# The later S5 parameter steps placed further on among the projections, and the first squares of x on ACT

## The chip, the cores and the metric

One core of a Trainium2 chip runs the whole program. The metric is the device time of one execution in microseconds; three executions of the kernel before were timed. PE is TensorE, DVE is VectorE, ACT is ScalarE, POOL is GpSimd, SP is SyncE, whose queue issues the loads.

## What is computed

A two-layer decoder trunk on 1024 tokens of width 1024, float32. Each layer normalises its input, projects it, runs four causal mixers of width 256 on parts of the projection, gates and merges them, projects the result and adds its norm to the input:

```python
h = _rms_norm(x, pre_g)
proj = jnp.einsum('bsd,dc->bsc', h, w_in)
...
y_ssm = s5_branch(ssm_u, ssm_a_re, ssm_a_im, ssm_log_dt, ssm_b_re, ssm_b_im, ...)
...
mix = jnp.stack([y_sb, y_ssm, y_ret, y_lru], axis=2)
mix = mix * jax.nn.silu(gates.reshape(bsz, s, N_BRANCH, BRANCH_WIDTH))
y = jnp.einsum('bsnw,nwd->bsnd', mix, w_branch)
merged = jnp.sum(jax.nn.sigmoid(merge) * y, axis=2)
return x + _rms_norm(jnp.einsum('bsd,de->bse', merged, w_out), post_g)
```

The mixers are stick-breaking attention, S5 (a complex diagonal state space with 16 groups), retention with rotary positions, and a gated linear recurrence (RG-LRU). S5 needs parameters that are worked out from `a`, `log_dt`, `b` and `c`: discretised poles, powers of them, multiplied `b` and `c`, and tables of rotations.

## The kernel before

The work is cut into four units: two layers, two chunks of 512 tokens each. A unit is a row of 64 **fillers**, which are the streamed projections: 0 to 15 make the mixers' inputs, 16 to 55 the gates, merges and branch projections (ten for each mixer), 56 to 63 the output projection. Each filler streams its weights from memory on SP's queue (`load_to`), and each half of a weight tile is split into a high part (`wh`, a copy on ACT, L86) and a low part (`wl`, a subtraction on DVE, L89), three halves ahead of its use (`split_to`, `ahead`). PE then makes three passes: high by high, low by high, high by low (`mm3`, L101). `pa` are the PSUM tiles of fillers, `pb` those of side tasks, `hh` and `hl` the split activations, `raw` the unsplit weights. `g` is any working tile of a common pool; its buffers are used in turn, so an instruction may wait until an earlier tile in the same buffer was read last.

Between the fillers run **side tasks**, written as generators: `first` (x of the first unit), `prep` (S5 parameters of a layer), `lru`, `s5`, `ret`, `sba`, `pro` (the next norm) and `post`. A hand-written table, `PLAN` (L1469), says at which half fillers of a unit each task takes its next step; an even number is before a filler, an odd one in its middle. All engines execute in the order that results, so an instruction which waits holds back everything behind it on its engine. `drain` finishes a task when a filler needs it.

`first` loads the eight tiles of x, multiplies each by its gain (ACT, L83) and makes the low part (`stt`, DVE, L98); squares of x are summed for the norm: POOL makes tiles 0 to 3 (L374) and adds them (L376), ACT makes 4 to 7, and DVE adds these four. Then POOL clears `tmat`, `ore` and `oim` (L1431).

`prep` runs on POOL for nearly all of its length (`ptt` L432, `pts` L436 and L438): exponentials, poles, their powers, `b` by the poles, then the rotation tables `tcos` and `tsin` by seven doublings, whose scratch `tmp` is a tile of the common pool. The steps behind them are:

```python
for src, dst in ((z4r, ore), (z4i, oim)):
    diag(src, dst)
...
            pe.transpose(ps[:, j * P:(j + 1) * P], src[:, 4 * h + j, :], ident)
        copy(dst[:, 4 * h:4 * h + 4, :], v3(ps[:, :], P))
```

that is two copies each into `ore` and `oim` (ACT), sixteen transposes (PE, L631) evacuated into `sre` and `sim` (ACT); then `wgh` and `wgl`, 24 products of `c` with the powers (POOL), a second `diag` of those into `ore` and `oim` (ACT), the lag matmuls (PE) and the DMAs into `tmat`. The task `s5` multiplies its input by `sre` and `sim` on PE and rotates the product by `tcos` and `tsin` on DVE, one half of the states after the other (the second half's first product writes a tile of the pool). `ret` multiplies its scores by the decay in `cons` and its queries by `xi` on DVE, multiplies both with values and states on PE for two pairs of heads in turn, and normalises the result over each head (two sums, squares on ACT, an inverse root, two products) before PE transposes it.

Of the kernel before, what the change touches and what calls it, by code (L numbers as in the profile page):

```python
# [28 lines left out]
# columns of the small parameter array  # L29
(C_CW, C_CB, C_BA, C_BX, C_LAM, C_BG, C_ARE, C_AIM, C_LDT, C_DSK, C_PG, NPAR) = (  # L30
    0, 8, 10, 12, 14, 16, 18, 26, 34, 42, 50, 58)
# columns of the constant array
# [11 lines left out]
def hybrid_kernel(ctx: ExitStack, tc: tile.TileContext, x, xt, ws1, ws2, par, bcw, preg, postg, con, rot, out, dbg=None):  # L44
# [107 lines left out]
    def group(u, i):  # L152
        # mixer of a filler in the order in which a unit takes them (LRU, S5, retention, attention by weights)
        return (0, 2, 1, 3)[(i - GATE0) // GRP] if u == 0 else (i - GATE0) // GRP

    def tile_of(u, i):
        # kind and place of the weights of a filler
        if i < GATE0:
            return 0, i
        if i >= WOUT0:  # L160
            return 0, i - 4 * 8
        n, j = group(u, i), (i - GATE0) % GRP
        return (1, 8 * n + j - 2) if j >= 2 else (0, GATE0 + 2 * n + j)
# [52 lines left out]
    S = {}  # L216

# [1 line left out]
    def prologue(u):  # L219
        l, c = units[u]  # L220
        src = x if l == 0 else x1
        gb = [G(), G()]
        xt = {}

        def load(t):
            xt[t] = [G(), G()]
            r0 = c * T + t * P
            for i in range(2):
                sp.dma_start(xt[t][i], src[r0:r0 + P, i * 512:(i + 1) * 512])

        st = smp.tile([P, 32], F32, tag="st", name=nm("st"))

        def square(t):
            junk = G(BF16)
            for i in range(2):
                actv(junk, xt[t][i], AF.Square, accum_out=st[:, 16 + 4 * i + t:17 + 4 * i + t])

        def scale(t0, n):
            # columns t0 .. t0 + n of the four blocks of st: v, 1/sqrt, scratch
            tt(st[:, t0:t0 + n], st[:, 16 + t0:16 + t0 + n], st[:, 20 + t0:20 + t0 + n], ALU.add)  # L240
            rstd(st[:, t0:t0 + n], st[:, 4 + t0:4 + t0 + n], st[:, 8 + t0:8 + t0 + n], D)

        def norm(t):
            for i in range(2):
                v = xt[t][i]
                stt(v, v, st[:, 4 + t:5 + t], gb[i], ALU.mult, ALU.mult)

        def flip(t):
            v = xt.pop(t)
            ps = [B(), B()]  # L250
            for q in range(2):
                for k in range(4):
                    pe.transpose(ps[q][:, k * P:(k + 1) * P], v[q][:, k * P:(k + 1) * P], ident)  # L253
            for q in range(2):
                pv = v3(ps[q][:, :], P)
                ho = hh[:, 4 * q:4 * q + 4, t * P:(t + 1) * P]
                copy(ho, pv)
                tt(hl[:, 4 * q:4 * q + 4, t * P:(t + 1) * P], pv, ho.bitcast(F32), ALU.subtract)
            Bdone(2)

        for t in range(NT):
            load(t)
        for i in range(2):
            sp.dma_start(gb[i], preg[l:l + 1, i * 512:(i + 1) * 512].partition_broadcast(P).rearrange("q o d -> q (o d)"))
        yield 0
        for t in range(NT):
            square(t)
            if t % 2:
                yield 0
        scale(0, 4)  # L270
        yield 0
        for t in range(NT):
            norm(t)
            if t % 2:
                yield HT + 2 if t + 1 == NT else 0
        hh = hp.tile([P, KD, T], F32R, tag="hh", name=nm("hh"))
        hl = hp.tile([P, KD, T], F32R, tag="hl", name=nm("hl"))
        for t in range(NT):
            flip(t)
            if t + 1 < NT:  # L280
                yield 2
        set_h(hh, hl)
# [4 lines left out]
    def token_rstd(acc):  # L287
        # 1/rms of token 4 p + t on partition p from sums over the other partitions
        st = smp.tile([P, 32], F32, tag="st", name=nm("st"))
        v, y, a = (st[:, 4 * i:4 * i + 4] for i in range(3))  # L290
        ps = B()
        for t in range(4):
            mm(ps[:, t:t + 1], acc[:, t:T:4], ones1)
        dve.tensor_copy(v, ps[:, 0:4])
        Bdone()
        rstd(v, y, a, D)
        return y

    def token_rows(y):
        # 1/rms of every token on all partitions  # L300
        ps = B()
        for t in range(4):
            mm(ps[:, t * P:(t + 1) * P], y[:, t:t + 1].to_broadcast([P, P]), ident)
        rb = G()
        copy(rb[:, :].rearrange("p (n t) -> p t n", t=4), v3(ps[:, :], P))
        Bdone()
        return rb

# [34 lines left out]
    def first():  # L343
# [19 lines left out]
        for k in range(KD):  # L363
# [8 lines left out]
            if k < 4:  # L372
                sqs.append(G())
                pool.tensor_tensor(sqs[k], xk[k], xk[k], op=ALU.mult)  # L374
                if k:
                    pool.tensor_tensor(sqs[0], sqs[0], sqs[k], op=ALU.add)  # L376
        S["h"] = (xh, xl)
        yield 0
        # statistics of the tokens
# [4 lines left out]
        for k in range(4, KD):  # L384
# [27 lines left out]
    def rstd(v, y, a, width):  # L412
        # v holds sums of squares; y receives 1/sqrt(mean + eps); a is scratch
# [3 lines left out]
    def rsqrt(v, y, a):  # L417
        # a bit-level first guess and three Newton steps; v becomes -v/2
# [26 lines left out]
    def exp_head(src, n, tmp):  # L445
        # 2^k factor (before its shift into the exponent) and the polynomial of the rest
# [22 lines left out]
    def prep(l):  # L469
# [18 lines left out]
        # exponentials for dt and softplus(-lambda)  # L488
# [14 lines left out]
        # discretised poles  # L503
# [20 lines left out]
        # softplus  # L524
# [30 lines left out]
        def cmul(zr, zi, ar, ai, br, bi, u1):  # L555
            # z = a * b ; u1 scratch
# [13 lines left out]
        # Bb and its multiples, for the chunk inputs  # L570
# [15 lines left out]
        def diag(src, dst):  # L586
            # (pair, t, channel) of the two groups of a pair on their rows into (pair, t, group, channel)
# [4 lines left out]
        # rotation tables by doubling  # L592
# [71 lines left out]
        # lag matrices  # L664
# [31 lines left out]
    def lru_weights():  # L696
        # high parts of a block's gate weights on all rows, low parts on its own ones
# [9 lines left out]
    def lru(l, c):  # L707
# [4 lines left out]
        for t in range(2):  # L712
# [7 lines left out]
            # high parts of a block on its own rows, low parts on the other ones  # L720
# [41 lines left out]
    def regroup(src, dst, buf, fold):  # L762
        # through memory: fold rows (pair, r), columns (t, k) into rows (t, r), columns (pair, k), or back
# [5 lines left out]
    def s5(l, c):  # L769
# [3 lines left out]
        # rows (t, channels of a pair), columns (pair, k)  # L773
# [26 lines left out]
        for h in range(2):  # L800
# [34 lines left out]
            if c == 0:  # L835
                # states carried to the next chunk
# [153 lines left out]
    def sba(l, c):  # L990
# [9 lines left out]
        for i in range(n + 3):  # L1000
            yield 3
            if i >= 2 and i - 2 < n and js[i - 2][1] % 2:
                # weights times values, two heads on the two column halves
# [22 lines left out]
            if i < n:  # L1026
                # logits of one head for 128 queries; the last 128 keys are masked by an added -1e30
# [19 lines left out]
            if i < n:  # L1047
                # w[s] = beta[s] * prod_{j > s} (1 - beta[j])
# [26 lines left out]
    def out_put(u, t, scaled):  # L1075
        # (t, 0) and (t, 1) times rstd, times the post-norm gain unless that is in them, plus the residual
# [34 lines left out]
    def mm3(ps, g, off, n, lhs_stat, hs, start, stop):  # L1111
        # one k-slice: three passes of split operands
# [231 lines left out]
    def evac_u(rb=None):  # L1344
        # tokens 4 k + t in the order (t, k)
# [76 lines left out]
    with tc.manual_schedule():  # L1422
# [9 lines left out]
        for u, (l, c) in enumerate(units):  # L1432
            for i in range(NTILE):
# [7 lines left out]
                for name, f in (("post", WOUT0), ("prep", NTILE if u else 24), ("lru", GATE0), ("s5", GATE0 + (1 if u else 2) * GRP),  # L1441
# [26 lines left out]
# half fillers (even: before one, odd: in its middle) at which the side tasks of a unit take their steps  # L1468
PLAN = [  # L1469
    {  # L1470
        "prep": (2, 3, 4, 6, 7, 10, 11, 13, 15, 16, 18, 19, 20, 25, 27, 28, 29, 30, 31, 32, 33, 37, 39, 41, 42, 44, 47),
        "lru": (12, 13, 14, 15, 17, 21, 28, 29),
        "s5": (31, 34, 35, 37, 38, 39, 40, 41, 42, 43, 44, 46, 47, 49, 51, 55, 56, 58, 59),
# [5 lines left out]
        "prep": (66, 67, 70, 72, 75, 76, 80, 81, 83, 85, 88, 89, 91, 93, 94, 95, 97, 99, 103, 104, 105, 107, 109, 110, 111, 112),  # L1479
# [21 lines left out]
def _pack(inp):  # L1501
# [4 lines left out]
    def cm(w, nk=KD):  # L1506
        # rows (k, p), 128 columns -> [p, k, cols]
# [6 lines left out]
    for l in range(DEPTH):  # L1514
# [45 lines left out]
        def gn(a):  # L1560
            # (16 groups, 64, ...) -> [(g2 n), p, ...]
# [9 lines left out]
        for n in range(4):  # L1571
            # gate weights of one block: (a, x) for even blocks, (x, a) for odd ones
# [47 lines left out]
```

## Time and profile before

| | |
|---|---|
| three timed executions | 1894.17, 1896.86, 1897.96 us; median 1896.86 |
| span of the profiled execution | 1895.3 us; its own time is not listed apart |
| PE busy | 1838.7 us, 97% |
| DVE, ACT, POOL busy | 62%, 48%, 13% |
| what ended PE's waits | ACT `wh` 27.4 us, DVE `wl` 8.2 us, DVE `g` (L98) 3.4 us |
| chain that ended last | PE 83%, POOL 8%, ACT 4%, DVE 3% |

All times of the views count from the start of the span. "Idle before" is the time in which an engine had nothing to run, with the instruction whose end released it. The chain is followed back from the last instruction to what released each step. The granted clock is given as a share of the full one.

### The profile page before, as it was taken

What the parts mean: (1) busy time and instruction counts of PE and PEld (TensorE: products, weight loads), DVE (VectorE), ACT (ScalarE), POOL (GpSimd) and SP (SyncE); (2) the same over time, 40 slices, a digit from 0 to 9 for tenths busy, and PEclk for the clock granted to TensorE, in tenths of its full rate; (3) what the DMA queues carried; (4) which work ended last, traced back from release to release, by engine and by line L of the source; (5) the groups of instructions that cost most, each with busy time, mean ns of one, the idle gap of its engine ahead of it and who ended that gap; (6) DMA issues with size and microseconds to landing.
All of it is one profiled execution on the core that took longest, in us unless ns stands there. A gap on an engine that the chain in (4) does not pass through costs nothing.

```text
span 1895.3 us, 24847 instructions
## 1 busy us (share of the span) xinstructions
PE 1838.7 (97%) x9210; PEld 1506.0 (79%) x9210; DVE 1180.3 (62%) x2101; ACT 903.4 (48%) x1733; POOL 252.1 (13%) x579
## 2 busy tenths in 40 slices
PE   8979999999989999979999999999999899999997
PEld 6768888888878878858888788888888788888886
DVE  7667755454669676735547956655537694776454
ACT  5862443344476443524446744344353855344333
POOL 7872000020000002880300000000000000000001
PEclk9989999999999999989999999999999999999999
DMA  5231232324332221314234313232243322212222
GB/s 181 90 104 56 68 117 98 122 93 152 106 117 95 100 72 58 108 47 150 96 127 156 115 69 109 78 137 99 90 136 131 103 98 87 81 68 78 97 98 105
DMA packets 68857, 193.96 MB, mean 102 GB/s; under 512 B 9600, under 2 KB 18176, under 8 KB 68736
## 3 DMA queue, kind: packets, MB, share of 16 engines
q1 hardware_dynamic: 68736, 192.38, 29.6%
q8 instruction: 72, 1.18, 0.2%
q14 instruction: 49, 0.40, 0.1%
HBM read 179.11 MB, written 12.58 MB: 101 GB/s over the span
## 4 chain that ended last, share of the span: by engine, by line
PE 83%; POOL 8%; ACT 4%; DVE 3%; issue 2%; DMA 0%; SPq 0%; DVEq 0%; POOLq 0%; ACTq 0%
PE pa L101 66%; PE pb L101 15%; POOL g L432 4%; ACT g L86 2%; PE pb L1020 2%; POOL psc L436 1%; DVE g L89 1%; POOL tcos L432 1%; POOL tsin L432 1%; POOL g L436 1%; ACT g L83 1%; DVE wl L89 1%; ACT wh L86 0%; DVE g L98 0%; PE pb L253 0%
## 5 line engine op out<-in xcount | busy, mean ns | idle before, releaser
L101 PE MATMUL pa<-hh,wh 128*128 128x512 f32 x1576 | 629.5, 399 | 27.4 <-ACT wh L86 27.4
L101 PE MATMUL pa<-hh,wl 128*128 128x512 f32 x1576 | 617.6, 392 | 8.0 <-DVE wl L89 8.0
L101 PE MATMUL pa<-hl,wh 128*128 128x512 f32 x1576 | 617.5, 392 | 0.0
L89 DVE TENSOR_TENSOR wl<-raw,wh 128x512 fp32r<-128x512 f32 (+1 forms) x512 | 373.8, 768 | 225.7 <-ACT wh L86 225.2
L89 DVE TENSOR_TENSOR g<-g,g 128x512 f32<-128x512 f32 (+7 forms) x432 | 296.0, 685 | 124.5 <-ACT g L86 104.6
L101 PEld LDWEIGHTS pa<-hh,wh 128*128 128x128 f32 x1576 | 298.9, 190 | 90.9 <-ACT wh L86 29.7
L86 ACT ACTIVATE wh<-raw 128x512 fp32r<-128x512 f32 (+1 forms) x512 | 328.2, 685 | 86.6 <-PE pb L101 41.0
L101 PEld LDWEIGHTS pa<-hh,wl 128*128 128x128 f32 x1576 | 298.0, 189 | 74.2 <-DVE wl L89 10.6
L101 PEld LDWEIGHTS pa<-hl,wh 128*128 128x128 f32 x1576 | 298.6, 189 | 58.4 <-DVE hl L89 0.2
L83 ACT ACTIVATE g<-pa 128x512 f32<-128x512 f32 x161 | 96.2, 597 | 501.0 <-PE pa L101 464.6
L89 DVE TENSOR_TENSOR g<-g,pa 128x512 f32<-128x512 f32 x128 | 87.6, 684 | 185.1 <-PE pa L101 165.8
L101 PE MATMUL pa<-g,wh 128*128 128x512 f32 x544 | 169.2, 391 | 3.6 <-DVE g L98 3.4
L86 ACT ACTIVATE g<-pb 128x512 f32<-128x512 f32 (+4 forms) x163 | 72.6, 472 | 145.8 <-PE pb L101 87.8
L906 POOL MEMSET g<- 128x512 f32 x8 | 4.0, 526 | 949.0 <-PE pb L101 947.8
L101 PEld LDWEIGHTS pa<-g,wh 128*128 128x128 f32 x544 | 102.1, 188 | 28.0 <-DVE g L98 5.0
L86 ACT ACTIVATE g<-g 128x512 fp32r<-128x512 f32 (+2 forms) x152 | 79.1, 521 | 61.7 <-DVE g L89 31.8
L86 ACT ACTIVATE g<-pa 64x128 fp32r<-64x128 f32 (+3 forms) x214 | 86.4, 404 | 45.2 <-PE pa L101 42.8
L101 PE MATMUL pa<-g,wl 128*128 128x512 f32 x272 | 106.1, 390 | 0.0
L83 ACT ACTIVATE g<-pb 128x512 f32<-128x512 f32 (+4 forms) x203 | 87.8, 513 | 22.8 <-PE pb L101 20.1
L101 PE MATMUL pa<-wh,g 128*128 128x512 f32 x256 | 79.6, 392 | 0.0
L101 PE MATMUL pb<-wh,g 128*128 128x512 f32 x256 | 79.2, 391 | 0.0
L89 DVE TENSOR_TENSOR g<-pa,g 128x512 f32<-128x512 f32 x51 | 35.7, 703 | 54.6 <-ACT g L83 34.8
(207 smaller groups left out, 2086.4 us busy)
## 6 DMA issues: line engine op xcount, KB each, us to landing
raw<-in_ws_dram SPq DMA_DIRECT2D x128, 640.0 KB, 3.8
raw<-in_ws_dram SPq DMA_DIRECT2D x127, 512.0 KB, 3.6
g<-x SPq DMA_DIRECT2D x32, 256.0 KB, 6.1
g<-in_xt_dram SPq DMA_DIRECT2D x16, 256.0 KB, 6.0
g<-in_x_dram SPq DMA_DIRECT2D x16, 256.0 KB, 3.1
x<-g SPq DMA_DIRECT2D x16, 256.0 KB, 2.1
out_dram<-g SPq DMA_DIRECT2D x16, 256.0 KB, 2.0
g<-in_rot_dram SPq DMA_DIRECT2D x8, 256.0 KB, 4.4
```

What stands on the lines that cost most here:

```text
L83: act.activation(out, in_, func, **kw)
L86: act.activation(out, in_, AF.Copy, **kw)
L89: dve.tensor_tensor(out, a, b, op=op)
L101: pe.matmul(out, lhsT=lhsT, rhs=rhs, start=start, stop=stop)
L432: pool.tensor_tensor(out, a, b, op=op)
L436: pool.tensor_scalar(out, a, s1, None, op0=op0)
L906: pool.memset(t, 0.0)
L1020: pe.transpose(ps[:, q * P:(q + 1) * P], r[:, q * P:(q + 1) * P], ident)
```

## The change

Three things. In `first`, POOL's four squares and three adds go; ACT makes the squares of tiles 0 to 3 inside the loop, and DVE adds seven tiles where it added four. In `PLAN`, the steps of `prep` from the copies into `ore` on move 6 to 7 half fillers on in unit 0 and 7 to 9 in unit 1, and the steps of `s5` in unit 0 from its third on move 6 (one of them 7). The point at which `prep` must be finished in unit 0 moves from filler 24 to 28. Comments are taken out; the numbers of lines fall by two behind `first`.

```diff
             if k < 4:
                 sqs.append(G())
-                pool.tensor_tensor(sqs[k], xk[k], xk[k], op=ALU.mult)
-                if k:
-                    pool.tensor_tensor(sqs[0], sqs[0], sqs[k], op=ALU.add)
+                actv(sqs[k], xk[k], AF.Square)
...
-        for k in range(4, KD):
+        for k in range(1, KD):
             tt(sqs[0], sqs[0], sqs[k], ALU.add)
...
-("prep", NTILE if u else 24)
+("prep", NTILE if u else 28)
...
-        "prep": (2, 3, 4, 6, 7, 10, 11, 13, 15, 16, 18, 19, 20, 25, 27, 28, 29, 30, 31, 32, 33, 37, 39, 41, 42, 44, 47),
+        "prep": (2, 3, 4, 6, 7, 10, 11, 13, 15, 16, 18, 19, 20, 25, 34, 35, 36, 37, 38, 39, 40, 44, 45, 47, 48, 50, 53),
...
-        "s5": (31, 34, 35, 37, 38, 39, 40, 41, 42, 43, 44, 46, 47, 49, 51, 55, 56, 58, 59),
+        "s5": (31, 34, 41, 43, 44, 45, 46, 47, 48, 49, 50, 52, 53, 55, 57, 61, 62, 64, 65),
...
-        "prep": (66, 67, 70, 72, 75, 76, 80, 81, 83, 85, 88, 89, 91, 93, 94, 95, 97, 99, 103, 104, 105, 107, 109, 110, 111, 112),
+        "prep": (66, 67, 70, 72, 75, 76, 80, 81, 83, 85, 88, 89, 91, 93, 103, 104, 105, 107, 110, 111, 112, 114, 116, 117, 118, 119),
```

ACT in unit 0, between the scores of attention (`pb`) and the rotary copies of the third projection (`g<-pa` in four pieces). Before:

```order
L86 ACTIVATE wh_1135<-raw_998 128x512
L86 ACTIVATE wh_1151<-raw_1052 128x512 [waits DMAHW6_49]
L86 ACTIVATE g_1169<-pa_1132 32x512 [waits PE_49]
L86 ACTIVATE g_1169<-pa_1132 32x512 x3
L86 ACTIVATE wh_1181<-raw_1052 128x512
L86 ACTIVATE wh_1197<-raw_1133 128x512 [waits DMAHW1_49,Activation_49]
L86 ACTIVATE ore<-g_638 64x32x16 [waits Pool_49]
L86 ACTIVATE ore<-g_638 64x32x16
L86 ACTIVATE oim<-g_639 64x32x16 [waits Pool_49]
L86 ACTIVATE oim<-g_639 64x32x16
L86 ACTIVATE g_1217<-pa_1178 32x512 [waits PE_49]
```

With the change:

```order
L86 ACTIVATE wh_1135<-raw_998 128x512
L86 ACTIVATE wh_1151<-raw_1052 128x512 [waits DMAHW6_49]
L86 ACTIVATE g_1169<-pa_1132 32x512 [waits PE_49]
L86 ACTIVATE g_1169<-pa_1132 32x512 x3
L86 ACTIVATE wh_1181<-raw_1052 128x512
L86 ACTIVATE wh_1197<-raw_1133 128x512 [waits DMAHW1_49,Activation_49]
L86 ACTIVATE g_1213<-pa_1178 32x512 [waits PE_49]
L86 ACTIVATE g_1213<-pa_1178 32x512 x3
L86 ACTIVATE g_1224<-pb_1222 128x128 [waits PE_49]
```

The copies into `ore` and `oim` have left this place, and the four evacuations into `sre` and `sim` that followed have too.

DVE in unit 0, at the same place (`cons` and `g` with 512 columns: the tables of the rotary positions and the products with them; the wait on `Pool` is for the buffer of the doublings' scratch). With the change:

```order
L89 TENSOR_TENSOR g_1170<-pa_1132,g_1128 128x512 [waits DMAHW7_49,PE_49,Activation_49]
L89 TENSOR_TENSOR g_1169<-g_1169,g_1129 128x512 [waits DMAHW0_49]
L89 TENSOR_TENSOR g_1170<-g_1170,g_1169 128x512 [waits DVE_49]
L89 TENSOR_TENSOR wl_1182<-raw_1052,wh_1181 128x512 [waits Activation_49]
L89 TENSOR_TENSOR wl_1198<-raw_1133,wh_1197 128x512 [waits DMAHW1_49,Activation_49]
L89 TENSOR_TENSOR g_1214<-pa_1178,g_1128 128x512 [waits PE_49,Activation_49,Pool_49]
L89 TENSOR_TENSOR g_1213<-g_1213,g_1129 128x512
L89 TENSOR_TENSOR g_1214<-g_1214,g_1213 128x512 [waits DVE_49]
L89 TENSOR_TENSOR wl_1245<-raw_1133,wh_1244 128x512 [waits Activation_49]
```

These rows, the wait included, are the same before and now but for the buffers' numbers.

DVE in unit 0, in retention (`cons` is the decay, and xi where no `pb` stands beside it; `g<-pb,tcos` begins a half of S5). Before, behind S5's second-half product and the first twelve of the sixteen products of retention's states:

```order
L98 SCALAR_TENSOR_TENSOR rcar<-g_1652,cons,pb_1689 64x64 [waits DVE_49] x4
L89 TENSOR_TENSOR wl_1728<-raw_1514,wh_1727 128x640
L89 TENSOR_TENSOR wl_1747<-raw_1597,wh_1746 128x640 [waits DMAHW2_49]
L1058 SCALAR_TENSOR_TENSOR g_1682<-g_1682,ones_118 128x255
L89 TENSOR_TENSOR g_1683<-g_1683,g_1682 128x255 [waits DVE_49]
L811 SCALAR_TENSOR_TENSOR g_1760<-s5s,g_1561 128x128 [waits DMAHW6_49,Activation_49]
L811 SCALAR_TENSOR_TENSOR g_1761<-s5s,g_1562 128x128
L811 SCALAR_TENSOR_TENSOR g_1760<-s5s,g_1561 128x128
L811 SCALAR_TENSOR_TENSOR g_1761<-s5s,g_1562 128x128
L89 TENSOR_TENSOR g_1776<-pb_1766,cons 128x512 [waits PE_49]
L89 TENSOR_TENSOR g_1778<-pb_1767,cons 128x512 [waits DVE_49]
L89 TENSOR_TENSOR g_1170<-g_1170,cons 128x512
```

With the change:

```order
L89 TENSOR_TENSOR g_1881<-pb_1871,tcos 128x512 [waits PE_49]
L89 TENSOR_TENSOR g_1883<-pb_1872,tsin 128x512 [waits DVE_49,PE_49]
L89 TENSOR_TENSOR g_1881<-g_1881,g_1883 128x512 [waits DVE_49]
L89 TENSOR_TENSOR g_1903<-g_1903,pa_1896 128x512 [waits Activation_49]
L89 TENSOR_TENSOR g_1882<-pb_1872,tcos 128x512 [waits Activation_49]
L89 TENSOR_TENSOR g_1883<-pb_1871,tsin 128x512 [waits DVE_49]
L89 TENSOR_TENSOR g_1882<-g_1882,g_1883 128x512 [waits DVE_49]
L89 TENSOR_TENSOR g_1919<-pb_1909,cons 128x512 [waits Activation_49]
L89 TENSOR_TENSOR g_1921<-pb_1910,cons 128x512 [waits DVE_49]
L89 TENSOR_TENSOR g_1283<-g_1283,cons 128x512
```

The small products of retention's states, two weight halves and four scans stood between S5's second-half product (now the three rows that begin with row five) and the products with `cons`; now nothing does.

## Rows read from the trace of the kernel before

**Rows 1.** The page: busy time, share and instructions of each engine
```profile
PE 1838.7 (97%) x9210; PEld 1506.0 (79%) x9210; DVE 1180.3 (62%) x2101; ACT 903.4 (48%) x1733; POOL 252.1 (13%) x579
```

**Rows 2.** PE's waits over the span: releaser, us in total, times, longest
```profile
PE pa L101 <- ACT wh L86: 27.4, 5, 13.4
PE pa L101 <- DVE wl L89: 8.2, 3, 7.8
PE pa L101 <- DVE g L98: 3.4, 3, 1.5
```

**Rows 3.** The chain of waits, 0 to 80 us: start, us, what
```profile
6.71 1.05 POOL g L374
...
18.41 1.94 POOL g L436 x2
```

**Rows 4.** The tile par, 0 to 30 us: its load, and issue to landing
```profile
L356 SPq DMA_DIRECT2D par<-in_par_dram x1: 653/653/653, 6.9 to 6.9; - x1
...
DMA to landing us min/median/max: 2.6/4.5/6.5
```

**Rows 5.** Timeline of DVE, 98 to 182 us: start, us, what [idle before]
```profile
116.41 0.69 DVE L89 TENSOR_TENSOR g<-pa,g 128x512 f32<-128x512 f32 x1 [14.70 <-POOL tsin L432]
```

**Rows 6.** Timeline of PE, 88 to 125 us
```profile
100.39 0.63 PE L631 MATMUL pb<-cons,ore 128*128 128x128 f32 x4 [1.66 <-POOL g L432]
...
119.12 0.79 PE L101 MATMUL pa<-hh,wl 128*128 128x512 f32 x1 [7.82 <-DVE wl L89]
```

**Rows 7.** Windows: us, PE, PEld, DVE, ACT, POOL busy, PEclk, DMA share, GB/s
```profile
15.00:20.00 5.00, 4.95 (x22) 3.78 (x21) 5.00 (x7) 4.20 (x8) 5.00 (x5) 1.00 0.86 324
105.00:110.00 5.00, 5.00 (x26) 4.10 (x25) 0.00 (x0) 4.97 (x8) 4.50 (x11) 1.00 0.00 0
```

**Rows 8.** Timeline of POOL, 17 to 42 us
```profile
22.65 0.52 POOL L436 TENSOR_SCALAR psc<-g 128x10 f32<-128x10 f32 x1
23.26 0.47 POOL L432 TENSOR_TENSOR g<-psc,g 128x10 f32<-128x10 f32 x1
...
28.09 0.21 POOL L432 TENSOR_TENSOR g<-psc,g 128x10 f32<-128x10 f32 x1
28.39 0.24 POOL L436 TENSOR_SCALAR psc<-g 128x10 f32<-128x10 f32 x1
```

**Rows 9.** Timeline of DVE, 157 to 178 us
```profile
159.51 0.69 DVE L89 TENSOR_TENSOR g<-pb,tcos 128x512 f32<-128x512 f32 x1 [3.73 <-ACT ore L86]
...
161.45 3.71 DVE L98 SCALAR_TENSOR_TENSOR g<-g,cons,pb 64x64 f32<-64x64 f32 x12
...
170.30 1.29 DVE L89 TENSOR_TENSOR g<-pb,cons 128x512 f32<-128x512 f32 x2
171.50 0.68 DVE L89 TENSOR_TENSOR g<-g,cons 128x512 f32<-128x512 f32 x1
```

**Rows 10.** Line L631, 85 to 125 us: xcount: ns min/median/max
```profile
L631 PE MATMUL pb<-cons,ore x8: 271/272/299, 100.4 to 104.0; 128*128 128x128 f32 x8
```

**Rows 11.** Timeline of PE, 155 to 182 us
```profile
172.24 4.78 PE L101 MATMUL pb<-g,g 128*128 128x128 f32 x24 [1.80 <-DVE g L89]
```

**Rows 12.** Windows, the stretch behind that wait, columns as above
```profile
172.90:179.80 6.90, 6.90 (x27) 6.32 (x27) 2.87 (x6) 2.43 (x4) 0.85 (x2) 0.51 0.00 0
```

**Rows 13.** Timeline of ACT, 118 to 182 us
```profile
156.42 0.66 ACT L83 ACTIVATE g<-pb 128x256 f32<-128x256 f32 x2 [0.94 <-PE pb L101]
...
158.22 1.26 ACT L86 ACTIVATE ore<-g 64x512 f32<-64x512 f32 x2
```

**Rows 14.** The chain of waits, 80 to 200 us
```profile
151.56 3.43 PE pa L101 x15
```

**Rows 15.** Timeline of DVE, 190 to 232 us
```profile
206.32 1.35 DVE L972 TENSOR_REDUCE rst<-g 128x8 f32<-128x512 f32 x2
...
214.50 1.29 DVE L89 TENSOR_TENSOR g<-g,rst 128x512 f32<-128x512 f32 x2
```

**Rows 16.** Timeline of ACT in unit 1, 835 to 862 us
```profile
846.62 1.08 ACT L86 ACTIVATE g<-pb 128x512 f32<-128x512 f32 x2 [23.47 <-POOL tsin L432]
```

More of the change, by code (lines that the diff above doesn't have):

```diff
@@ L1440, in hybrid_kernel @@
                     load_par(l + 1)
-                for name, f in (("post", WOUT0), ("prep", NTILE if u else 24), ("lru", GATE0), ("s5", GATE0 + (1 if u else 2) * GRP),
+                for name, f in (("post", WOUT0), ("prep", NTILE if u else 28), ("lru", GATE0), ("s5", GATE0 + (1 if u else 2) * GRP),
                                 ("ret", GATE0 + (2 if u else 1) * GRP), ("sb", GATE0 + 3 * GRP)):
```

## The prediction

> **What bounds the kernel now.** I read the engine shares first: PE is busy 97% of a span of 1895.3 us, so the time changes by what PE waits for, by what it runs extra, and by the stretches in which its clock falls [rows 1]. The list of PE's waits comes second [rows 2]: 27.4 us in five waits for a high half of the weights, the longest 13.4 us, and 8.2 us for a low half, of which one wait is 7.8 us. Everything else is small. The third view is the chain of waits, which says what stood behind the 7.8 us: in the first 116 us the chain runs on POOL almost alone, from the first square of x at 6.71 us on [rows 3].
>
> **The chain in unit 0.** POOL makes three squares-and-adds and a fourth square, clears `tmat`, `ore` and `oim`, and starts the S5 parameters only at 18.39 us. The parameter columns that this first operation reads are issued at 6.9 us and land 6.5 us later, so they were there at 13.4 us [rows 4]. From there POOL runs on to the last `tsin` product. DVE waits 14.70 us for it, because its next rotary product writes into the buffer that the doubling used as scratch [rows 5]; the low halves of the weights are queued behind that product, and PE loses 7.82 us for them [rows 6].
>
> **The change, part by part.**
>
> **1. Squares to ACT.** Seven POOL operations leave (four squares, three adds). The three memsets read nothing, so POOL can run them before the parameters land, and the first parameter operation moves from 18.39 to 13.43 us: 4.96 us earlier. That isn't yet 4.96 us at the end of the chain. DVE is busy 5.00 of 5.00 us between 15 and 20 us, but 0.00 between 105 and 110, where the tables are finished [rows 7]. Beside a busy DVE small POOL operations start 0.61 us apart, alone 0.30 us [rows 8]. So the 4.96 us hold about 8 operations, and each saves 0.30 us at the far end: 8 x 0.30 = 2.5 us. The bounds are 4.96 (the chain shifts rigidly) and 1.0 (the three adds that DVE gets slow POOL by most of the rest). I take **-2.5 us**, since the end of the chain lies beside an idle DVE.
>
> The Trainium skill speaks against more than that: "SBUF — State Buffer", "Who interferes with whom", says that a DVE instruction with two SBUF inputs and a GpSimd instruction that reads SBUF exclude each other, and the second waits out the whole first. By that rule each small operation would wait out one DVE operation; with 0.69 us for one [rows 9] that is 7 operations in 4.96 us, an estimate of -2.1 us in place of -2.5, and a sum of +3.05. The spacing of 0.61 us leans that way without showing the lock.
>
> PE's early waits for the low part of x, 3.4 us in three, go too, since DVE no longer works beside long POOL operations [rows 2]. I count them as **0**: PE then reaches the wait for the tables 3.4 us sooner and waits 3.4 us longer. What hides them is that wait; without it they would be worth 3.4 us. The four squares on ACT (0.55 us each) and three adds on DVE lie in the same cover.
>
> The Trainium skill, "Perfetto Trace Analysis", "Optimizing Scalar/DVE Operations", recommends moving work to Scalar when DVE is saturated and warns of the port that GpSimd and DVE share. By that alone the 3.4 us would come off the time and the sum below would end at -0.75; the chain, in which POOL stands without a gap, says otherwise.
>
> **2. The parameter steps of unit 0, 6 to 7 half fillers later.** The order of DVE shows the same rotary product with the same wait on POOL, so the wait stays and only moves with the chain. What moves past it are ACT's `ore` and `oim` copies, PE's 16 transposes and four evacuations. Before, the transposes lay in front of the stall, where PE had time, and the 1.66 us that PE waited for the first of them lay there too [rows 6]; both were free. Now the transposes come behind it. One transpose lasts 0.27 us and four take 0.63, so four occupy 0.63 - 0.27 = 0.36 us, and sixteen **+1.45 us** [rows 6, 10]. ACT's own copies are off PE's path there.
>
> **3. S5 and C of unit 0, 6 half fillers later.** Before, the second-half product of S5 waited for ACT's `ore` copies [rows 9], sixteen small products of retention followed on DVE, and PE waited 1.80 us for the second retention product [rows 11]. Right behind it the granted clock was 0.51, the lower of the two levels, for 6.9 us [rows 12], which costs half of them, 3.4. With the sixteen products now well ahead, both go: **-5.2 us**.
>
> In their place the second-half product again stands behind ACT's copies of `ore` and `oim`, and now the *third* and *fourth* scores of retention and the xi product are right behind it on DVE, without the sixteen. What PE waits for next is the end of this chain: on ACT sigmoid, two weight copies, two `ore` copies, 3.1 us from 156.42 to 159.5 [rows 13]; on DVE three products, 159.51 to 161.45, and three more, about 1.9 us from 170.30 on [rows 9]. Together 3.1 + 1.9 + 1.9 = 6.9 us against 15 matmuls in between, 3.43 us [rows 14]: a new wait of **+3.5 us**. The bound below is 0 (PE comes to it late enough), above 5.2 (half of the matmuls run before the sigmoid has its input).
>
> The retention norm moves relative to the lag matmuls too: its squares now use a buffer that the second lag product frees, and the transposes of the output come 30 matmuls later, 6.9 us at the pace of those 15 [rows 14]. DVE ran from 206.32 to 215.2 us, 8.9 us, between the sums of the squares and the first scaled output [rows 15]. That is **+2.0 us**, between 0 and 2.7. The first retention product may wait up to 1.5 us for POOL's products of C; PE has about as much work, so 0.
>
> Whether the clock falls again is the one choice that isn't from a sum. It fell after 7.82 and 1.80 us of waiting, and not after 1.66. A wait of 3.5 us is nearer to the first two, so I count one such stretch again, **+3.4 us**; none and two are the bounds.
>
> **4. Unit 1, 7 to 9 half fillers later.** ACT waits 23.47 us there for `tsin` [rows 16], and PE 13.4 us behind it [rows 2]. The steps up to the tables keep their numbers and the order of ACT is the same up to that copy: **0**. The moved steps land on PE, ACT and POOL where PE has a filler in hand: 0, within 1 either way.
>
> **Sum:** -2.5 + 1.45 - 5.2 + 3.5 + 2.0 + 3.4 = +2.65. The span of the profile lies 1.6 us under the median of the runs, 1896.86; the difference is added to the median: 1896.86 + 2.65 = **1899.5 us**.
>
> **The rivals.**
> A, faster. PE reaches the second retention product so late that ACT and DVE are ready, and the new waits do not arise. For it speaks that DVE has lost the sixteen products there, against it the 6.9 us of chain against 3.43. Without 3.5, 2.0 and 3.4 the sum is -6.25: 1890.6.
> B, slower. The new wait at the second retention product, with POOL's start worth only 1.0. It decides if ACT's copies of C stand on the path there for more than 1.8 us, the wait after which the clock fell before; then a second stretch follows the norm's wait, and the first retention product waits its 1.5: -1.0 + 1.45 - 5.2 + 3.5 + 2.0 + 1.5 + 6.8 = +9.05, 1905.9.
> C, nothing happens. POOL's head start is eaten by DVE's adds, and the later waits change places one for one: 1.45, so 1898.3.
> D. The 13.4 us of unit 1 go as well, because less stands on ACT before them. The order speaks against it, nothing for it: 1899.5 - 13.4 = 1886.1.
>
> **How the numbers follow.** Forecast 0.43, A 0.22, B 0.20, C 0.10, D 0.05. A measurement of this kernel can tell 0.2% from no change, 3.8 us, which is 1893.1 to 1900.7. The forecast's own range, with the terms of part 1, the norm or the second wait one at a time at their bounds, is 1896 to 1902.5, so 0.31 of it count as the same and 0.12 as slower. Faster: A and D, 0.27. Same: 0.31 + C = 0.41. Slower: 0.12 + B = 0.32. The range goes from A to B, 1890 to 1906; it leaves out D and the outer parts of A and B.
>
> **What would show it.** In the new profile: no squares on POOL and its first parameter operation near 13.4 us; the tables done near 114; PE's wait for a low half still there near 109 to 117, now longer; no 1.80 us wait before a x24 product near 172 but one of about 3.5 us before the second such product, 20 us on; the transposes behind the long wait; unit 1's 13.4 us unchanged. It is wrong if the wait of unit 1 is gone, if the tables are done 5 us earlier, or if no wait over 1 us stands between 160 and 220 us.

## The result and the profile after

The changed kernel takes 1911.65 us (median of four, 1909.31 to 1912.66) against 1897.13 of the kernel before (1894.17 to 1897.96): a ratio of 1.0081, interval 1.0068 to 1.0093. It is slower by 14.5 us between the medians, where 2.65 were forecast, and above the range. The page of the profile after, its span and engine shares:

```profile
span 1910.9 us, 24848 instructions
...
PE 1846.7 (97%) x9210; PEld 1511.8 (79%) x9210; DVE 1176.3 (62%) x2104; ACT 903.8 (47%) x1737; POOL 240.7 (13%) x572
```
PE is still busy 97% of the span, and the share hides the loss. PE's waits after (releaser, us in total, times, longest), beside [rows 2]:

```profile
PE pa L101 <- ACT wh L86: 28.0, 7, 13.3
PE pa L101 <- DVE wl L89: 10.1, 2, 9.9
PE pb L101 <- DVE g L89: 4.4, 3, 3.4
PE pb L101 <- ACT ore L86: 3.5, 1, 3.5
PE pb L981 <- DVE g L89: 2.5, 1, 2.5
```
The wait for a low half grew from 8.2 to 10.1 us, the one in unit 1 for a high half is as long as before, and three waits are new or longer: 3.4 us for a product of retention (the longest of the third row), 3.5 us for `ore`, 2.5 us for the norm.

To see where the time is lost, the matmuls with streamed weights were paired in order, 6912 in either trace; the start of the same matmul in both tells how far the changed kernel is ahead or behind. The steps from row to row say more than a single row, since traces of kernels with the same code up to the first row differ there by 0.9 us (below):

| the matmul | before | after | behind |
|---|---|---|---|
| behind the long wait of unit 0 | 119.12 us | 118.27 us | -0.85 us |
| the 811th; the distance then stays near 7 us | 257.92 | 264.81 | +6.9 |
| behind the long wait of unit 1 | 848.38 | 855.83 | +7.45 |
| unit 1, before the lag products | 921.58 | 927.90 | +6.3 |
| unit 1, behind them | 944.98 | 960.17 | +15.2 |
| the last | 1883.41 | 1899.04 | +15.6 |

There are two losses: about 8 us in unit 0 behind the tables, and 8 to 9 us in the last fillers of unit 1.

**The start.** POOL's first parameter operation in the trace after, its next small ones, and DVE's adds:

```profile
13.81 1.38 POOL L434 TENSOR_SCALAR g<-par 128x2 f32<-128x2 f32 x2 [10.36 <-DMA par<-in_par_dram]
...
19.16 0.65 POOL L434 TENSOR_SCALAR psc<-g 128x10 f32<-128x10 f32 x1
19.89 0.66 POOL L430 TENSOR_TENSOR g<-psc,g 128x10 f32<-128x10 f32 x1
...
28.80 0.24 POOL L434 TENSOR_SCALAR psc<-g 128x10 f32<-128x10 f32 x1
29.13 0.20 POOL L430 TENSOR_TENSOR g<-psc,g 128x10 f32<-128x10 f32 x1
```
```profile
17.56 5.31 DVE L89 TENSOR_TENSOR g<-g,g 128x512 f32<-128x512 f32 x7
```
POOL begins at 13.81 us where it began at 18.41 [rows 3]. But beside DVE's seven adds small operations start 0.73 us apart, against 0.33 us when DVE does little. Of the lead of 4.6 us, 0.85 is left at the tables between these two traces, and PE waits 9.88 us where it waited 7.82 [rows 5, 6]:

```profile
115.56 0.69 DVE L89 TENSOR_TENSOR g<-pa,g 128x512 f32<-128x512 f32 x1 [13.82 <-POOL tsin L430]
```
```profile
118.27 0.80 PE L101 MATMUL pa<-hh,wl 128*128 128x512 f32 x1 [9.88 <-DVE wl L89]
```
Two traces are too few for the 0.85, as the experiments below show. In the five traces with the same code up to here and the squares on POOL (before, e2, e3, e8, e9) DVE's product behind the tables starts at 116.41 to 117.33 us, 116.95 in the mean; in the four with the squares on ACT (after, e1, e4, e5) at 114.86 to 115.58, 115.33 in the mean. POOL's first operation moved by 5.05 us in these means, so about 1.6 of 5.05 us are left. And the longer wait of PE isn't due to the squares: in e2, without them, it is 9.9 us, in e1, with them alone, 6.9. It belongs to the steps of unit 0: the transposes and PE's wait of 1.66 us for them no longer stand ahead of it.

**Unit 0, retention.** The transposes run behind the long wait now (PE, the first of four groups):

```profile
132.14 0.60 PE L629 MATMUL pb<-cons,ore 128*128 128x128 f32 x4
```
Then ACT in the trace after, around the second scores and at the norm's squares:

```profile
184.51 0.60 ACT L83 ACTIVATE g<-pa 128x512 f32<-128x512 f32 x1 [7.89 <-PE pb L101]
...
186.26 1.26 ACT L86 ACTIVATE ore<-g 64x512 f32<-64x512 f32 x2
...
212.20 1.16 ACT L83 ACTIVATE g<-g 128x512 f32<-128x512 f32 x2 [8.11 <-PE pb L101]
```
DVE beside it, the second half of S5, the products with `cons`, and the norm's sums and scaling:

```profile
187.55 0.69 DVE L89 TENSOR_TENSOR g<-pb,tcos 128x512 f32<-128x512 f32 x1 [1.73 <-ACT ore L86]
...
190.69 0.68 DVE L89 TENSOR_TENSOR g<-g,cons 128x512 f32<-128x512 f32 x1
...
212.87 1.28 DVE L970 TENSOR_REDUCE rst<-g 128x8 f32<-128x512 f32 x2 [6.63 <-ACT g L83]
...
221.12 1.29 DVE L89 TENSOR_TENSOR g<-g,rst 128x512 f32<-128x512 f32 x2
```
And PE's two waits at the end of these chains:

```profile
191.42 4.35 PE L101 MATMUL pb<-g,g 128*128 128x128 f32 x24 [3.35 <-DVE g L89]
```
```profile
221.95 1.23 PE L981 MATMUL pb<-cons,g 128*128 128x128 f32 x8 [2.48 <-DVE g L89]
```
From the sigmoid at 184.51 to the retention product at 191.42 it is 6.9 us of ACT and DVE work without a gap that matters, against 15 matmuls; PE waits 3.35 us. The norm's squares wait 8.11 us for PE's lag products; from the sums at 212.87 to the first scaled output, which the transposes need, 8.9 us pass, and PE waits 2.48 us.

The granted clock behind these waits and behind those of unit 1 (windows; us, busy of PE, PEld, DVE, ACT, POOL, then the clock, DMA share, GB/s):

```profile
191.40:200.00 8.60, 8.58 (x36) 7.67 (x37) 2.82 (x6) 0.93 (x2) 0.00 (x0) 0.60 0.22 78
222.00:227.00 5.00, 5.00 (x26) 3.90 (x27) 4.83 (x19) 2.96 (x7) 0.00 (x0) 0.66 0.02 3
951.90:957.30 5.40, 4.60 (x31) 3.82 (x32) 4.85 (x8) 2.12 (x4) 0.16 (x1) 0.51 0.30 93
```
0.60 over 8.6 us, 0.66 over 5.0 and 0.51 over 5.4 cost 3.4, 1.7 and 2.6 us beside a full clock. The timed executions show it too: their granted clock is 0.983 of the full one in the mean of the four, and 0.987 in 15 of the kernel before. One minus the clock, times the span, is 32.9 against 24.6 us, so by this estimate some 8 of the 14.5 us are clock (a little less where PE waited at the low clock anyway).

**Unit 1.** SP's queue between 880 and 960 us, what it waited for, and its issues:

```profile
SPq L1284 <- POOL g L430: 29.2, 1, 29.2
```
```profile
942.33 0.80 SPq L1284 DMA_DIRECT2D g<-in_postg_dram  x2
943.18 15.79 SPq L178 DMA_DIRECT2D raw<-in_ws_dram  x6
```
ACT and PE there:

```profile
948.80 1.93 ACT L86 ACTIVATE wh<-raw 128x512 fp32r<-128x512 f32 x3 [12.91 <-DMA raw<-in_ws_dram]
950.63 1.25 ACT L86 ACTIVATE ore<-g 64x512 f32<-64x512 f32 x2
```
```profile
951.93 0.53 PE L101 MATMUL pb<-ore,g 128*32 128x96 f32 x2 [3.51 <-ACT ore L86]
```
L1284 loads the post-norm gain with filler 56. Its buffer is one that POOL's products of C (of `c` with the powers) hold, so it stands for 29.2 us until 942.33, and the weights of the next fillers stand behind it in the queue. In the kernel before the same load stood there too, until PE released it, and PE waited for nothing between 880 and 960 us:

```profile
SPq L1286 <- PE pa L101: 19.1, 1, 19.1
```
So the standing of 19.1 us was covered, and the 10 us on top of it were not. In the changed kernel ACT waits 12.91 us for those weights; its copies into `ore` and `oim` are queued behind three halves of them; PE waits 3.51 us for the first and 0.76 for the second. POOL's part of C had ended at 943.9 us, 6.7 us before the first copy.

### The profile page after: what moved, and what is told of

Same layout as the page of the kernel before. It is cut to its first block, busy times and chain, and to the rows that moved or that the text cites. A ratio compares the mean times of both kernels' runs of the same rounds, so it can differ in the third digit from the quotient of the medians.

```text
span 1910.9 us, 24848 instructions
## 1 busy us (share of the span) xinstructions
PE 1846.7 (97%) x9210; PEld 1511.8 (79%) x9210; DVE 1176.3 (62%) x2104; ACT 903.8 (47%) x1737; POOL 240.7 (13%) x572
## 4 chain that ended last, share of the span: by engine, by line
PE 80%; POOL 8%; issue 5%; ACT 4%; DVE 2%; DMA 1%; SPq 0%; DVEq 0%; POOLq 0%; ACTq 0%
PE pa L101 62%; PE pb L101 15%; POOL g L430 4%; ACT g L86 2%; PE pb L1018 2%; POOL psc L434 1%; POOL tcos L430 1%; POOL tsin L430 1%; DVE g L89 1%; POOL g L434 1%; ACT g L83 1%; ACT wh L86 0%; PE pb L253 0%; DMA par<-in_par_dram 0%; ACT L83 0%
## 5 line engine op out<-in xcount | busy, mean ns | idle before, releaser
L101 PE MATMUL pa<-hh,wl 128*128 128x512 f32 x1576 | 618.8, 393 | 10.1 <-DVE wl L89 9.9
L83 ACT ACTIVATE g<-g 128x512 f32<-128x512 f32 (+2 forms) x98 | 56.8, 600 | 31.3 <-DVE g L89 17.3
```

The source lines that it names most:

```text
L83: act.activation(out, in_, func, **kw)
L101: pe.matmul(out, lhsT=lhsT, rhs=rhs, start=start, stop=stop)
```

## The experiments

Ratios and medians stand against runs of the kernel before on the same chip. Its medians on the chips used lie between 1895.4 and 1897.1 us, so times of different groups can be set beside each other to some 2 us. A first group takes the change apart, a second takes away one suspected cause each, the last puts together what paid.

**e1, the squares alone.**

```diff
-                pool.tensor_tensor(sqs[k], xk[k], xk[k], op=ALU.mult)
...
+                actv(sqs[k], xk[k], AF.Square)
...
```

> Only the squares of x go to ACT and the adds to DVE; the table of steps stays that of before. Theory (three separate parts): POOL begins the parameters about 4.6 us sooner, has 0.9 to 1.3 us of that left at the last table, so 1 us less than before: 1896, and the wait behind the tables starts where it did. Rival (the squares carry the loss: ACT and DVE are late in the first 20 us and the clock falls there): 3 us or more over before.

1893.85 us against 1895.84, ratio 0.9990 (0.9982 to 0.9999). The squares pay 2 us, and the loss isn't theirs. PE's wait at the tables is shorter than before (PE's waits), and its wait of 1.80 us of [rows 11] is there, with no fall of the clock behind it:

```profile
PE pa L101 <- DVE wl L89: 7.3, 3, 6.9
```
```profile
170.29 2.89 PE L101 MATMUL pb<-g,g 128*128 128x128 f32 x24 [1.80 <-DVE g L89]
```
```profile
165.00:185.00 20.00, 18.20 (x119) 14.99 (x119) 15.50 (x40) 6.58 (x13) 1.31 (x3) 1.00 0.21 67
```
The product takes 2.89 us where it took 4.78, and the clock is 1.00 from 165 to 185 us. That is one execution: over the eleven timed ones the granted clock is 0.9865 in the mean, against 0.9870 in the 15 of the kernel before. So the two microseconds do not come from the clock; the 1.6 us left at the tables account for them within the interval.

**e2, unit 0 alone.**

```diff
-... ("prep", NTILE if u else 24), ...
+... ("prep", NTILE if u else 28), ...
...
-        "prep": (... 25, 27, 28, 29, 30, 31, 32, 33, 37, 39, 41, 42, 44, 47),
+        "prep": (... 25, 34, 35, 36, 37, 38, 39, 40, 44, 45, 47, 48, 50, 53),
...
-        "s5": (31, 34, 35, 37, 38, 39, 40, 41, 42, 43, 44, 46, 47, 49, 51, 55, 56, 58, 59),
+        "s5": (31, 34, 41, 43, 44, 45, 46, 47, 48, 49, 50, 52, 53, 55, 57, 61, 62, 64, 65),
```

> Only unit 0's steps move (prep, s5, the drain). Theory: the waits of 3.4 us at the second retention product and 2.5 us at the retention norm come with this part alone, with a lower clock behind them, and the 1.8 us wait of before goes: 7 to 9 us over before, about 1905. Rival (these waits need POOL's head start too, or the squares cost): within 3 us of before.

1905.54 against 1895.84, 1.0053 (1.0040 to 1.0065): 9.7 us. Both waits are there without the squares, and so is the longer one at the tables (PE's waits of this run):

```profile
PE pa L101 <- DVE wl L89: 10.2, 3, 9.9
PE pb L101 <- DVE g L89: 4.4, 3, 3.4
...
PE pb L983 <- DVE g L89: 2.5, 1, 2.5
```
The granted clock of its five executions is 0.984 in the mean, against 0.987: by the estimate used above 5.8 of the 9.7 us.

**e3, unit 1 alone.**

```diff
-        "prep": (... 91, 93, 94, 95, 97, 99, 103, 104, 105, 107, 109, 110, 111, 112),
+        "prep": (... 91, 93, 103, 104, 105, 107, 110, 111, 112, 114, 116, 117, 118, 119),
```

> Only unit 1's steps move. Theory: the load of the post-norm gain stands on SP's queue behind POOL's products of C, the next weights behind it, ACT's copies into ore and oim behind those, and PE waits 3.5 + 0.8 us with a lower clock behind it: 6 to 8 us over before, about 1904. Rival (unit 1 loses only because unit 0 left it later): within 1 us of before.

1904.14 against 1895.84, 1.0043 (1.0030 to 1.0055): 8.3 us, and the wait for `ore` is there:

```profile
PE pb L101 <- ACT ore L86: 3.6, 1, 3.6
```
**e4, squares and unit 0, unit 1 as before.**

> The whole change without unit 1's steps. Theory (the parts add): 7 us less than the whole change, 1904 to 1905. Rival (unit 1's loss is there without its moved steps): 1910 or more.

1904.93, 1.0047 (1.0033 to 1.0061): 9.1 us over before. The parts add within their intervals: -2.0 + 9.7 + 8.3 = 16 us against 14.5 measured for the whole. With unit 0 moved the squares are worth 0.6 us (e2 to e4), which these runs can't tell from nothing.

**e5, the post-norm gain later in unit 1.**

```diff
-            if j == 0:
+            if j == (6 if u == 1 else 0):
                 S["postg"] = [G(), G()]
```

> The whole change, but in unit 1 the post-norm gain is loaded six fillers later (with filler 62 instead of 56). Theory (unit 1's loss is SP's queue: the weights stand behind a load that waits for POOL's products): the 12.9 us wait of ACT for weights and PE's 3.5 and 0.8 us waits for ore and oim go, so 6 to 8 us less than the whole change, 1903 to 1905. Rival (ACT's copies into ore and oim are late because POOL's products are): the waits stay, 1909 or more.

1903.09, against 1911.65 of the whole change. SP waits 0.6 us for that load now, and PE's two waits for `ore` and `oim` are not in its list any more:

```profile
SPq L1284 <- PE pb L101: 0.6, 1, 0.6
```
POOL and ACT do the same work at the same fillers, so the queue was the cause.

**e6, the scratch of the tables, kernel before.**

```diff
-        t1, t2 = tmp, sc2
+        t1 = sre[:, :, :].rearrange("p a b -> p (a b)")
```

> The kernel before, with the tables' doubling using sre as scratch, so that no rotary product waits for the buffer. Theory (both long waits are only that buffer): PE's 7.8 us in unit 0 and 13.4 us in unit 1 go with the lower clock behind them, 20 to 26 us under before, 1870 to 1876. Rival (something else that needs the tables is next, S5's rotation or POOL's other buffers): each wait only moves, at most 8 us gained, 1888 or more.

1884.88 against 1895.94, 0.9941 (0.9927 to 0.9956): half of what was expected. Unit 1's wait is gone. In unit 0 the edit made a wait of its own, since ACT wants to evacuate the transposes into `sre` before the tables are done (ACT, then PE):

```profile
117.57 0.60 ACT L86 ACTIVATE sre<-pb 128x512 f32<-128x512 f32 x1 [12.55 <-POOL tsin L432]
```
```profile
123.64 0.80 PE L101 MATMUL pa<-hh,wh 128*128 128x512 f32 x1 [12.62 <-ACT wh L86]
```
**e7, the same scratch, the whole change.**

> The whole change with the same scratch. Theory (the buffer is the wait, the later steps give the tables time): both long waits go and the losses that the moved steps brought stay: 20 to 26 us under the whole change, 1886 to 1892. Rival (the later steps are what the tables needed once the buffer is free, and their losses were only the price of the wait): under 1880, below e6. Second rival: the waits move, 1900 or more.

1890.33 against 1895.94, 0.9968 (0.9956 to 0.9979), 21.3 us under the whole change. Here the transposes come after the tables, so nothing waits for `sre`; 3.5 us are left of the wait in unit 0, and the one in unit 1 is gone. Both long waits are one buffer; the later steps did not remove them, and their own losses stay.

**e8, S5 of unit 0 alone.** The line of `s5` in the table, and nothing else.

> The kernel before, with only s5 of unit 0 moved 6 half fillers; prep stays. Theory (the 3.4 us wait at the second retention product comes from ACT's copies of C that stand ahead of S5's second-half product): without them there the chain is 4.5 us against 3.4 us of PE, a wait of about 1 us, and no transposes behind the long wait: 1 to 4 us over before. Rival (moving S5 behind the retention states is itself the loss): wait of 3 us or more, 6 to 9 us over before.

1893.38 against 1895.94, 0.9986 (0.9977 to 0.9996): 2.6 us faster, where 1 to 4 over were expected. Moving S5 behind the states of retention does what part 3 of the prediction took off, and the new waits come only with `prep` (PE's waits):

```profile
PE pb L101 <- DVE g L89: 1.0, 2, 0.5
```
**e9, C two half fillers earlier, unit 0 as in the change** (the table against that of e2; the rest is as in e2).

```diff
-        "prep": (... 34, 35, 36, 37, 38, 39, 40, 44, 45, 47, 48, 50, 53),
+        "prep": (... 34, 35, 36, 37, 38, 39, 40, 42, 43, 45, 48, 50, 53),
```

> Only unit 0's steps move, as in e2, but C's last two products and ACT's copies of them come two half fillers earlier, ahead of the sigmoid. Theory (the 3.4 us wait is the sigmoid, two weight copies and two ore copies in one row): two ore copies, 1.25 us, and the wait of S5's product on them leave the row, so PE's wait falls to 0.5 to 1.5 us, with less low clock behind it: 2 to 5 us under e2, 1901 to 1903; the norm's 2.5 us stays. Rival (the wait comes from DVE's order alone): 3 us or more remain, within 1 us of e2.

1899.56 against 1895.43, 1.0018 (1.0008 to 1.0027), 6 us under unit 0 alone and 1.4 under the range expected. The 3.4 us wait has gone, the norm's stays, and the clock between 185 and 200 us is full:

```profile
PE pb L983 <- DVE g L89: 2.5, 1, 2.5
...
PE pb L101 <- DVE g L89: 1.0, 2, 0.5
```
```profile
185.00:200.00 15.00, 15.00 (x110) 12.74 (x109) 11.09 (x23) 2.94 (x7) 1.27 (x2) 1.00 0.13 45
```
**e10, scratch in `tmat`, kernel before.**

```diff
-        t1, t2 = tmp, sc2
+        t1 = tmat[:, 0:4, :].rearrange("p a b -> p (a b)")
...
+        pool.memset(tmat[:, 0:4, :], 0.0)
```

> The kernel before, the doubling's scratch in tmat, cleared again by POOL. In e6 the scratch was sre, which ACT wants to fill before the tables are done. Theory: unit 0's long wait goes with it, 6 to 10 us under e6, 1875 to 1879. Rival (the tables themselves, or the other buffers of the parameter task, stop PE in unit 0 a few fillers later): within 3 us of e6, 1882 to 1888.

1878.26 against 1895.43, 0.9905 (0.9890 to 0.9919). Of 13.4 and 7.8 us, 4.3 are left in unit 0 (PE's waits, then DVE):

```profile
PE pa L101 <- DVE wl L89: 5.5, 4, 4.3
```
```profile
111.37 2.87 DVE L89 TENSOR_TENSOR wl<-raw,wh 128x512 fp32r<-128x512 f32 x2 [4.12 <-ACT wh L86]
```
DVE waits for no buffer there; it is busy without a pause from 111.4 us on, and beside POOL's last products two low halves take 2.87 us, where two behind the tables of the kernel before took 1.28 with POOL idle. I read that rest as the two engines beside each other; it was not tried apart.

**e11, what paid, together:** `tmat` as scratch, squares on ACT, S5 of unit 0 moved, `prep` as before.

> The kernel before with tmat as scratch, the squares on ACT, and s5 of unit 0 moved, prep not moved. Theory (what paid alone pays together): 2 for the squares, 2.5 for s5 under e10, 1870 to 1876. Rival (with the long wait gone PE's early gain no longer hides, or S5 comes too early for the tables): 1866 or less, or no gain over e10.

1874.05 against 1895.43, 0.9883 (0.9868 to 0.9897), 4.2 us under the scratch alone.

**e12, the whole change with its losses taken away:** gain later, C earlier, `tmat` as scratch.

> The whole change with its losses taken away one by one: the post-norm gain later in unit 1, C two half fillers earlier in unit 0, tmat as scratch. Theory (the losses found are all there is): 1890 of e7 less 8 for unit 1 and 3 for C, 1877 to 1881, near e10. Rival (more losses behind): 1885 or more.

1874.27, 0.9886 (0.9870 to 0.9903). It is 37 us under the change as it stands and as fast as the version before it. Both beat both kernels. It came out below its range, by 2.7 us; which part gave that was not tried apart. The norm's wait is still there, but in this execution the clock behind it did not fall, where it was 0.72 over 6 us in e9 (PE's row, then the window):

```profile
206.87 1.23 PE L982 MATMUL pb<-cons,g 128*128 128x128 f32 x8 [2.48 <-DVE g L89]
```
```profile
207.00:213.00 6.00, 6.00 (x38) 4.79 (x38) 5.83 (x20) 2.98 (x7) 0.00 (x0) 1.00 0.07 6
```

## Why the prediction was wrong

**Part 4, unit 1, is the step that failed.** "The moved steps land on PE, ACT and POOL where PE has a filler in hand: 0, within 1 either way." It measured +8.3 us alone (e3), and e5, which moves only the load, takes 8.6 us off the whole change. The three engines were looked at and SP's queue was not: a step moved later holds its buffers later, and the first to ask for one of them was a load, with the weights of every later filler behind it. The trace of before already had that load standing in the queue for 19.1 us. This term alone puts the time out of the range: 1899.5 + 8.3 = 1907.8 us, against an upper end of 1906.

**Part 1, the squares.** -2.5 us forecast at the tables (8 x 0.30 is 2.4), about 1.6 measured over the traces and 2.0 us of kernel time in e1: nearly right, and between its bounds. The lead at the first operation was as forecast (5.05 against 4.96); the spacing beside DVE was 0.73, not 0.61 us, and DVE was busy there for longer, with three more adds. The rule of the Trainium skill on the port that DVE and GpSimd share ("SBUF — State Buffer", "Who interferes with whom") gave -2.1, nearer; the spacing of 0.73 us, about one DVE operation, agrees with it. PE's early waits did not all go: those for DVE fell from 3.4 to 0.6 us, but 1.2 us of waiting for ACT came in their place (1.5 in e1). That the tables cover them held, since the 2.0 us of e1 (0.2 to 3.4 by its interval) are about what the tables gave; but PE's wait there became shorter, 6.9 us, and not longer. The advice of the Trainium skill, "Perfetto Trace Analysis", "Optimizing Scalar/DVE Operations", to move work to Scalar where DVE is saturated, read as 3.4 us off the time, did not decide here; no run shows the early waits apart.

**Part 2, the transposes.** Their four groups stand behind the long wait, as forecast, the first of 0.60 us. The forecast of 1.45 us was not measured apart.

**Part 3, unit 0.** The waits were right: 3.5 us forecast at the second retention product and 3.35 measured, with the same chain of 6.9 us; 2.0 at the norm and 2.48 measured. The clock is the second step that failed: 3.4 us won and 3.4 lost were to cancel, and in e2 the timed executions lost some 5.8 us more to the clock than before (the estimate above). Two waits, not one, brought a low clock, 3.4 and 1.7 us. And the 5.2 us that left were not all sure: in e1, e6 and e10 the same 1.80 us wait has no low clock behind it, and in e3, whose code is the same up to there, it costs half as much as before. Parts 2 and 3 come to +5.15 us in the sum and to 9.7 in e2. Which wait each part caused is shown by e2, e8 and e9: S5's move gains, C's copies on ACT cost the first wait. That the norm's wait comes from the buffer of its squares is read from the order and from ACT's 8.11 us; it was not tried alone.

**The rivals.** B, slower by +9.05, had the right sign and the right mechanism in unit 0 (two waits, a low clock behind each) and nothing of unit 1. That e4, without unit 1, gives 9.1 us is partly luck: B's 1.5 us at the first retention product did not come. A fell with the 3.35 us wait. C fell with 14.5 us. D fell: the wait of 13.3 us in unit 1 is unchanged, and e6, e7 and e10 show that another buffer for the scratch removes it.

## What to carry to other kernels

When a task is moved in a hand-written order, follow its buffers as well as its instructions: list who takes each buffer next, and on which queue that one stands, loads first, since a load that waits for a buffer holds every load behind it. How long it stands decides: 19.1 us cost nothing here, 29.2 us cost 8.3. When an engine waits for a long task, see whether it needs the result or only a buffer that the task holds; here another tile as scratch was worth 17 us (e10) and the reordering cost 14.5. And cost each part of a change by itself: here two moves paid by themselves (the squares 2.0 us, S5 of unit 0 2.6 us), and the losses of the others hid them.

## What was not expected of the hardware

The granted clock did not fall each time after the same wait: behind PE's 1.80 us wait it was 0.51 for 6.9 us in the profile of before [rows 12], 1.00 in e1, e6 and e10, and 0.91 on average from 165 to 185 us in e3. Behind the waits of 3.35 us in the change and in e2 it fell (0.60 and 0.58 over 8 us). Behind the 2.5 us of the norm it fell in the change, e2 and e9 (0.66, 0.62, and 0.72 over 6 us) and not in e12 (1.00 over 6 us). A sum that counts such a stretch once as lost and once as won carries some 3 us that one trace can't settle; the clock of many timed executions is the better witness. Small operations on POOL start 0.73 us apart beside DVE's adds and 0.33 apart without them, so that 5.05 us of lead there were worth 1.6 in the means.
